# The first stage of a two-layer encoder step written as one list of steps over all engines

## The chip, the core and the metric

The kernel runs on one core of a Trainium2 chip. The core has engines that each take their own instructions in order: TensorE (PE in the profile; its weight loads are PEld), VectorE (DVE), ScalarE (ACT), GpSimd (POOL) and SyncE (SP). DMA transfers are issued by an engine and wait in that engine's queue (SPq, ACTq, POOLq). The metric is the device time of one execution in microseconds (us), the median over runs.

## The reference

One inference step of a two-layer encoder for 1024 prompt frames and 32 sample frames of width 1024, all in f32. Each layer makes modulation vectors from a condition, normalizes, mixes, and runs a feed-forward part:

```python
mod = jax.nn.silu(c) @ w_ada[i] + b_ada[i]              # 1024 -> 6 x 1024, for 2 conditions
sh1, sc1, gt1, sh2, sc2, gt2 = jnp.split(mod[:, None, :], N_MOD, axis=-1)
h = rmsnorm(x, g_norm[i, 0]) * (1 + sc1) + sh1
...
z = jax.nn.gelu(h @ w_in)                               # layer 0: spatial gating, 1024 -> 2 x 2048
u, v = jnp.split(z, 2, axis=-1)
v = rmsnorm(v, g_v)
...
x = x + gt1 * rmsnorm(mix, g_norm[i, 1])
h = rmsnorm(x, g_norm[i, 2]) * (1 + sc2) + sh2
f = jnp.square(jax.nn.relu(h @ ffn_w_up[i])) @ ffn_w_down[i]
x = x + gt2 * rmsnorm(f, g_norm[i, 3])
```

The stage that the change touches reads x, makes the first h of layer 0 out of it (with sh1 and sc1, the first 2048 of w_ada's 6144 columns), and begins the product of h with the v half of w_in.

## The kernel before

**Tiles.** The 1056 frames are nine blocks of 128 rows (the ninth has 32) in three tiles: blocks 0 to 2, 3 to 5, and 6 to 8. A tile lies transposed in `acc[t]`: model channels on the partitions, in eight groups of 128 (k = 0 to 7), frames along the row. Matmuls run on f32 values split in two: `wh` and `hh` are the rounded parts (type fp32r), `wl` and `hl` what is left. A product is three passes: hh by wh, hl by wh, hh by wl.

**The stream.** `stream` is the list of all loads from memory in the order in which they are issued, each 512 KB: blocks of x, pieces of w_ada and pieces of the weights. `issue()` (L395) sends them to SP's queue as long as slots are free, except that block 2 of x goes to ACT's queue; `stream_to(kind, key)` (L949) lets the kernel take up loads until the one named. The first 26 are three blocks of x, then four rounds q = 0 to 3 of four w_ada pieces (name `ada`) and one weight piece `("v", 0, q)`; x3 to x5 stand behind the weight piece of round 0.

**The first stage** stands in a part in which the program fixes the order itself (L991, `tc.manual_schedule()`). What it holds, for each engine:

- Small vectors (L180, `load_vectors`): g_norm, b_ada, pool_scale, g_v and the two conditions are loaded as rows through ACT's queue (tiles `row0` to `row2`) and turned on PE into columns (`csilT` for the conditions behind a Silu on ACT, `rowT` for the others).
- `x_squares` (L565): ACT squares a block and sums it, the sums go into `ssx`. `x_turn` (L580): PE transposes a block in two halves of four 128x128 transposes (`xT`), and VectorE or ACT (L588) copies each into `acc`.
- `do_ada_pe` (L477): PE multiplies a w_ada piece by the conditions (`ada0_0` to `ada0_7`; two pieces of four matmuls for each), VectorE turns the sums (`adas`), PE gathers them (`adat`, L459), and VectorE adds the bias (coefficients and shifts).
- `spread` (L715): from the sums of squares, VectorE makes the mean (`ms`), ACT takes a square root and VectorE a reciprocal (L722, L723), three VectorE steps refine it, ACT makes three diagonals (L730, `r_h`), and PE spreads them over the partitions (`pb`, L732).
- `apply`: for each k, VectorE multiplies `acc` by coefficient and factor (`mt`), ACT adds the shift and rounds (`hh`, L875), VectorE makes the rest (`hl`).
- `do_w`: ACT rounds a weight piece (`wh`, L422), VectorE subtracts (`wl`, L79).
- `early_mm(bs, q)` (L961, matmul at L973): the products of blocks bs by weight piece q into five PSUM tiles `pv0_0` to `pv0_4`, 120 matmuls in all.

The program writes these in whole pieces: all of tile 0's two k of a round, then `early_mm((0, 1, 2), q)`, then tile 1's two k, then `early_mm((3,), q)` and `early_mm((4,), q)`. Behind the last round, PE turns blocks 6 to 8, the third tile is normalized in the same way, and the stage of v follows: weight pieces `("v", 1, q)`, matmuls at L929 to L931, gelu (L941). `sgu_group` (L1142) belongs to the stage behind that: its small matrices `wt` and `bs` are loaded through SP's and ACT's queues as soon as a slot is free, the first two at the start of the program.

Of the kernel before, what the change touches and what calls it, by code (L numbers as in the profile page):

```python
# [34 lines left out]
def tile_stream_encoder_step(  # L35
# [154 lines left out]

    def turn_conditions():
        raw = vec_rows[2]
        nc.vector.memset(csil32, 0.0)
        act(out=raw[0:16, P : 2 * P], in_=raw[0:16, :P], func=AF.Silu)

        act(out=raw[0:16, 2 * P : 2 * P + 1], in_=epsT[0:16, :], func=AF.Sqrt)
        pt = ps_ms("csilT")
        nc.tensor.transpose(pt[:, 0:16], raw[0:16, P : 2 * P], ident[0:16, 0:16])
        nc.vector.tensor_copy(csil, pt[:, 0:16].rearrange("p (v k) -> p k v", v=NV))
        nc.vector.tensor_copy(csil32[:, :, 0:NV], csil)  # L200

    def turn_vectors():
        for raw, v in zip(vec_rows, vecs):
            n = v.shape[1]
            pt = ps_ms("rowT")
            nc.tensor.transpose(pt[:, :n], raw[:n, :P], ident[:n, :n])
            nc.vector.tensor_copy(v, pt[:, :n])
# [187 lines left out]
    def issue():  # L395
        while state["issued"] < len(stream):
# [22 lines left out]
    def do_w(key, r):  # L419
# [4 lines left out]
        if key == ("v", 0, 0):  # L424
            late_lo.append(lambda: tt(out=wl, in0=r, in1=wh.bitcast(F32), op=ALU.subtract))
        else:
            tt(out=wl, in0=r, in1=wh.bitcast(F32), op=ALU.subtract)


    late_lo = []  # L430
# [38 lines left out]

    pe_folds = []  # L470

    def do_ada_pe(l, sl, q, r):
        if q == 0:
            ada_acc[0] = ps_ms(f"ada{l}_{sl}")
        pa = ada_acc[0]
        for c in range(4):
            mm(  # L477
                pa[32 * c : 32 * c + 32, :256],
                csil32[:, 4 * q + c, :],
                r[:, c * 256 : (c + 1) * 256],  # L480
                start=q == 0,
                stop=q == 1,
                tile_position=(0, 32 * c),
                skip_group_check=True,
            )
        if q == 0:
            return
        s = t_m(f"adas{l}_{sl}")
        nc.vector.transpose(out=s[:, :256], in_=pa[:, :256])

        def fold():
            x = s[:, :256].rearrange("p (h a j) -> p a h j", h=2, a=4)
            pb = gather(f"adat{l}_{sl}", [x[:, a, :, 0:NV] for a in range(4)])
            ada_finish(
                l, sl // 4, 2 * (sl % 4), pb[:, : 2 * NV].rearrange("p (k v) -> p k v", v=NV)
            )

        pe_folds.append(fold)
# [73 lines left out]
    def x_turn(b, r):  # L572
# [3 lines left out]
        for half in range(2):  # L576
# [6 lines left out]
            dst = acc[t][:, half * 4 : half * 4 + 4, HALO + c0 : HALO + c0 + nr]  # L583
            src = pt[:, : 4 * nr].rearrange("p (a b) -> p a b", a=4)
            if half == 0 or t == 0:
                nc.vector.tensor_copy(dst, src)
            else:
                act(out=dst, in_=src, func=AF.Copy)  # L588
# [4 lines left out]
    def do_x(b, r):  # L593
        x_squares(b, r)
        if b < 3:
            x_turn(b, r)
        else:
            x_turns.append(lambda: x_turn(b, r))
# [10 lines left out]
    def stream_step():  # L609
# [10 lines left out]
        elif kind == "ada":  # L620
            if k < first_ada:
                do_ada_pe(*key, r)
            else:
                do_ada(*key, r, 256)
        else:
            do_x(key, r)
# [88 lines left out]
    def spread(t, ss, tag, out, dg):  # L715
# [6 lines left out]
        act(out=r0[:, :nb], in_=ms[:, :nb], func=AF.Sqrt)  # L722
        nc.vector.reciprocal(out=r0[:, :nb], in_=r0[:, :nb])  # L723
# [234 lines left out]
    early_ps = [(ps_dn if b < 3 else ps_up)(f"pv0_{b}") for b in range(5)]  # L958
    h0, h1, h2 = (first_norm(t) for t in range(NT))

    def early_mm(bs, q):  # L961

        wh, wl = witem[("v", 0, q)]
        for second in (False, True):
            for b in bs:
                t, c0 = b // 3, b % 3 * P
                tick(0.46 if second else 0.92)
                for k in range(2):
                    kb = 2 * q + k
                    a_h, a_l = hh[t][:, kb, c0 : c0 + P], hl[t][:, kb, c0 : c0 + P]  # L970
                    w = slice(k * 512, k * 512 + 512)
                    for a in (a_h,) if second else (a_h, a_l):
                        mm(  # L973
                            early_ps[b],
                            a,
                            (wl if second else wh)[:, w],
                            start=kb == 0 and a is a_h and not second,
# [696 lines left out]
```

## Time and profile before

| | |
|---|---|
| median of 3 runs | 2169.93 us (2169.7 to 2171.16) |
| the profiled execution: time | 2173.74 us |
| its span, from the first to the last instruction | 2171.7 us |
| TensorE clock granted, mean | 0.996 of full speed |
| busy over the span | PE 99%, PEld 96%, DVE 66%, ACT 45%, POOL 1% |
| bytes moved | 312.95 MB, mean 144 GB/s |

The page names groups of instructions by line, engine and operation, and by the tiles they write and read (`out<-in`); `x16` is a count. A view over stretches of time gives, for each engine, the busy time in the stretch with the number of instructions, and then the granted clock, the share of time in which the DMA engines were busy and their GB/s. The order of its engine columns is PE, PEld, DVE, ACT, POOL. A timeline gives for a window the start and the length of each group of instructions that stand together.

### The profile page before, as it was taken

To read this page: it belongs to the slowest core of one execution; us is meant where nothing else is said; L and a number is where in the kernel's file an instruction comes from. 1 tells how busy PE (TensorE), PEld (TensorE's weight loads), DVE (VectorE), ACT (ScalarE), POOL (GpSimd) and SP (SyncE) were. 2 spreads that over 40 slices of the span, in tenths; PEclk is the share of its full clock that TensorE was granted. 3 is DMA by queue.
4 is the path that set the end of the run, shared out by engine and by line. 5 is a ranking of instruction groups with operands and counts; after the bars stand their busy time and mean duration, and the time that the engine had idled before them with its cause. 6 is when DMAs were issued, how large, how long until landed. Compare 5 with 4: busy or idle time off the path is not lost.

```text
span 2171.7 us, 33210 instructions
## 1 busy us (share of the span) xinstructions
PE 2145.5 (99%) x13214; PEld 2078.1 (96%) x13214; DVE 1431.8 (66%) x2499; ACT 971.3 (45%) x1643; POOL 13.3 (1%) x30
## 2 busy tenths in 40 slices
PE   7999999999999999999999999999999999999998
PEld 5778899999999999999999999999999999999997
DVE  5688647566879548496747879869675554523377
ACT  4633422234447552323445566666555542313354
POOL 0000000000000000000000000000000000000001
PEclk9999999999999999999999999999999999999999
DMA  8386534343437454243645466565455552302255
GB/s 300 119 269 193 173 93 139 90 148 109 147 96 233 132 155 143 87 140 110 196 129 161 141 189 182 171 191 158 141 161 158 157 155 68 98 20 78 69 139 125
DMA packets 383262, 312.95 MB, mean 144 GB/s; under 512 B 39458, under 2 KB 346346, under 8 KB 383108
## 3 DMA queue, kind: packets, MB, share of 16 engines
q1 hardware_dynamic: 380452, 308.64, 46.8%
q8 instruction: 103, 1.69, 0.3%
q10 hardware_dynamic: 2144, 1.41, 0.2%
q0 software_dynamic: 512, 0.79, 0.1%
q14 instruction: 51, 0.42, 0.1%
HBM read 278.95 MB, written 31.84 MB: 143 GB/s over the span
## 4 chain that ended last, share of the span: by engine, by line
PE 93%; DVE 3%; DMA 2%; ACT 1%; issue 1%; ACTq 0%; DVEq 0%; SPq 0%
PE pg L902 11%; PE pg L903 11%; PE pg L904 11%; PE pf L902 11%; PE pf L904 11%; PE pf L903 11%; PE po L902 3%; PE po L903 3%; PE po L904 3%; PE pu L902 3%; PE pu L904 3%; PE pu L903 3%; PE pv L929 2%; PE pv L930 2%; PE pv L931 2%; PE pp L1532 1%
## 5 line engine op out<-in xcount | busy, mean ns | idle before, releaser
L902 PE MATMUL pg<-fh,wh_dn 128*128 128x384 f32 (+1 forms) x1536 | 495.8, 323 | 0.0
L902 PE MATMUL pf<-hh,wh_up 128*128 128x384 f32 (+1 forms) x1536 | 494.4, 322 | 0.0
L903 PE MATMUL pf<-hl,wh_up 128*128 128x384 f32 (+1 forms) x1536 | 493.1, 321 | 0.0
L904 PE MATMUL pf<-hh,wl_up 128*128 128x384 f32 (+1 forms) x1536 | 492.9, 321 | 0.2 <-DVE wl_up L79 0.2
L903 PE MATMUL pg<-fl,wh_dn 128*128 128x384 f32 (+1 forms) x1536 | 492.6, 321 | 0.4 <-DVE fl L79 0.4
L904 PE MATMUL pg<-fh,wl_dn 128*128 128x384 f32 (+1 forms) x1536 | 492.5, 321 | 0.0
L79 DVE TENSOR_TENSOR wl_up<-raw,wh_up 128x1024 fp32r<-128x1024 f32 x152 | 185.9, 1224 | 165.4 <-ACT wh_up L422 165.4
L902 PEld LDWEIGHTS pg<-fh,wh_dn 128*128 128x128 f32 x1536 | 288.3, 188 | 1.5 <-ACT fh L1121 0.6
L903 PEld LDWEIGHTS pg<-fl,wh_dn 128*128 128x128 f32 x1536 | 288.3, 188 | 1.5 <-DVE fl L79 0.7
L904 PEld LDWEIGHTS pf<-hh,wl_up 128*128 128x128 f32 x1536 | 288.6, 188 | 0.5 <-DVE wl_up L79 0.5
L903 PEld LDWEIGHTS pf<-hl,wh_up 128*128 128x128 f32 x1536 | 288.3, 188 | 0.4
L902 PEld LDWEIGHTS pf<-hh,wh_up 128*128 128x128 f32 x1536 | 288.2, 188 | 0.4
L904 PEld LDWEIGHTS pg<-fh,wl_dn 128*128 128x128 f32 x1536 | 288.3, 188 | 0.0
L422 ACT ACTIVATE wh_up<-raw 128x1024 fp32r<-128x1024 f32 x152 | 161.2, 1060 | 279.9 <-PE pf L903 213.6
L79 DVE TENSOR_TENSOR acc<-acc,pg 128x384 f32<-128x384 f32 (+1 forms) x336 | 174.2, 519 | 146.3 <-PE pg L904 145.7
L422 ACT ACTIVATE wh_dn<-raw 128x1024 fp32r<-128x1024 f32 x152 | 160.8, 1059 | 202.9 <-PE pg L903 170.6
L79 DVE TENSOR_TENSOR wl_dn<-raw,wh_dn 128x1024 fp32r<-128x1024 f32 x152 | 186.0, 1224 | 82.4 <-ACT wh_dn L422 82.2
L79 DVE SCALAR_TENSOR_TENSOR aa<-raw,csil,aa 128x512 f32<-128x512 f32 (+1 forms) x364 | 203.5, 623 | 8.0 <-DMA raw<-in_w_ada_dram 7.9
L1295 ACT ACTIVATE r<-pf 128x384 f32<-128x384 f32 (+1 forms) x192 | 86.6, 451 | 201.9 <-PE pf L904 199.2
L79 DVE TENSOR_TENSOR fl<-r,fh 128x384 fp32r<-128x384 f32 (+1 forms) x192 | 100.3, 523 | 85.4 <-ACT fh L1121 84.3
L902 PE MATMUL pu<-hh,wh_u 128*128 128x384 f32 (+1 forms) x384 | 125.8, 328 | 0.0
L902 PE MATMUL po<-ush,wh_o 128*128 128x384 f32 (+1 forms) x384 | 123.5, 322 | 0.0
(263 smaller groups left out, 2927.2 us busy)
## 6 DMA issues: line engine op xcount, KB each, us to landing
raw<-in_ffn_w_up_dram SPq DMA_DIRECT2D x152, 512.0 KB, 3.9
raw<-in_ffn_w_down_dram SPq DMA_DIRECT2D x152, 512.0 KB, 3.5
raw<-in_w_ada_dram SPq DMA_DIRECT2D x96, 512.0 KB, 4.3
raw<-in_sgu_w_in_dram SPq DMA_DIRECT2D x40, 512.0 KB, 4.4
xd<-acc SPq DMA_DIRECT2D x8, 1536.0 KB, 7.8
raw<-in_sgu_w_out_dram SPq DMA_DIRECT2D x24, 512.0 KB, 4.0
xo_r<-xd SPq DMA_DIRECT2D x32, 384.0 KB, 3.4
vd<-vt SPq DMA_DIRECT2D x32, 256.0 KB, 4.5
```

What stands on the lines that cost most here:

```text
L79: return op(out, *args, **kw)
L422: act(out=wh, in_=r, func=AF.Copy)
L902: mm(ps[:, :n], wh, rh, start=i == 0, stop=False)
L903: mm(ps[:, :n], wh, rl, start=False, stop=False)
L904: mm(ps[:, :n], wl, rh, start=False, stop=i == last)
L929: mm(ps[:m, :], a_h, wh[:, o : o + 512], start=k == 0, stop=False)
L930: mm(ps[:m, :], a_h, wl[:, o : o + 512], start=False, stop=False)
L931: mm(ps[:m, :], a_l, wh[:, o : o + 512], start=False, stop=k == KB - 1)
L1295: act(out=r[:, :n], in_=ps[:, :n], func=AF.Relu)
L1532: mm(ps[:, :n], wg[:, k, e * P : (e + 1) * P], A(t, 2 * g + k), start=k == 0, stop=k == 1)
```

## The change

The stage's pieces are broken into single steps, and the order of all of them is one list of words, `order`. Each word is a step with its numbers: `mt1_3` is mt of tile 1, k = 3; `hh` and `hl` likewise; `xT4_0` the first half of block 4's transposes and `xc4_0` its copy; `ada6_1` the second piece of ada 6; `g0_3`, `h0_3` and `l0_1` are the three passes hh by wh, hl by wh (for one k) and hh by wl (for two k) of block 0. A loop takes the words in order and calls the step's function, so that each engine's instructions stand in the order of the list. The list has 255 words (100 of them `g`, `h` and `l`) and ends with the squares of blocks 6 to 8; blocks 6 to 8 are turned behind it, as before.

Beside the order, these things change:

- `warm(12)` stands ahead of the list and four `warm` words in it (seven more matmuls): a 128x512 product of ones into a PSUM tile whose value nobody reads.
- x3 to x5 stand in the stream behind the weight piece of round 1 instead of round 0; block 2 of x goes to SP's queue like the others.
- g_norm, b_ada, pool_scale and g_v are loaded through GpSimd's queue; the conditions stay on ACT's.
- `spread` takes the inverse square root in one ACT instruction (Abs_reciprocal_sqrt), without VectorE's reciprocal. Two small ACT instructions ahead of their use take the functions' tables.
- The copies of the second halves of tile 1's and 2's blocks are on ACT, as before.
- `wt` and `bs` of `sgu_group` are issued only behind the load of `("v", 2, 3)`, and `bs` goes to SP's queue.

```diff
@@ load_vectors
-    def load_vectors(i, part):
+    def load_vectors(queue, i, part):
         at = sum(k for _, k in rows[i][: part.start])
         for ap, k in rows[i][part]:
-            nc.scalar.dma_start(vec_rows[i][at : at + k, :P], ap)
+            queue.dma_start(vec_rows[i][at : at + k, :P], ap)
...
@@ the stream
         add_w(*v_item(0, q))
-        if q == 0:
+        if q == 1:
             for b in range(3, 6):
                 add_x(b)
...
-                i = (nc.scalar if key == 2 else nc.sync).dma_start(
+                i = nc.sync.dma_start(
...
@@ spread
-        act(out=r0[:, :nb], in_=ms[:, :nb], func=AF.Sqrt)
-        nc.vector.reciprocal(out=r0[:, :nb], in_=r0[:, :nb])
+        act(out=r0[:, :nb], in_=ms[:, :nb], func=AF.Abs_reciprocal_sqrt)
...
@@ the first stage
-    def early_mm(bs, q):
...
+    def warm(n):
+        w = slot("pv0_2", lambda: ps_dn("pv0_2")) if "vec2" in held else slot("warm", lambda: ps_up("warm"))
+        for _ in range(n):
+            mm(w.rearrange("p (a b) -> p a b", a=4), onesr, fresh, start=True, stop=True)
...
+    def xT(b, half):
+        pt = slot(f"xT{b}_{half}", lambda: ps_ms(f"xT{b}_{half}"))
+        for i in range(4):
+            nc.tensor.transpose(
+                pt[:, i * P : (i + 1) * P], got("x", b)[:, half * 4 + i, :], ident
+            )
...
+    def high(b, k, part=None):
+        t, c0 = b // 3, b % 3 * P
+        tick(0.23)
+        w = witem[("v", 0, k // 2)][0][:, k % 2 * 512 : k % 2 * 512 + 512]
+        pv(b, (hl if part is None else part)[t][:, k, c0 : c0 + P], w)
+
+    def low(b, q):
+        t, c0 = b // 3, b % 3 * P
+        tick(0.46)
+        for k in range(2):
+            w = witem[("v", 0, q)][1][:, k * 512 : k * 512 + 512]
+            pv(b, hh[t][:, 2 * q + k, c0 : c0 + P], w)
...
+    order = """
+        silu xT0_0 xsq0 csilT xT0_1 xc0_0 csil xsq1 xT1_0 xc0_1 rowT0 xT1_1 vec0 xc1_0 xsq2 xT2_0
...
+        hh0_3 ms1 xc3_1 g2_3 hl0_3 g0_3 rs1 g1_3 xc4_1 xT5_0 nr1 ada6_0 xc5_0 dg1 ada6_1 ada2_0
...
     with tc.manual_schedule():
-        load_vectors(2, slice(0, 2))
+        load_vectors(nc.scalar, 2, slice(0, 2))
         issue()
-        load_vectors(2, slice(2, 4))
-        load_vectors(0, slice(0, 1))
-        load_vectors(1, slice(0, 1))
-        turn_conditions()
-        stream_to("x", 1)
-        turn_vectors()
...
+        load_vectors(nc.gpsimd, 0, slice(0, 1))
+        load_vectors(nc.gpsimd, 1, slice(0, 1))
+        load_vectors(nc.gpsimd, 2, slice(2, 4))
+        act(out=vec_rows[2][64:80, P : P + 1], in_=epsT[64:80, :], func=AF.Silu)
+        nc.vector.memset(csil32, 0.0)
+        warm(12)
+        for step in order.split():
+            name = step if step in steps else step.rstrip("0123456789_")
+            steps[name](*(int(i) for i in step[len(name) :].split("_") if i))
+        for b in (6, 7, 8):
+            x_turns.append(lambda b=b: x_turn(b, got("x", b)))
...
@@ sgu_group
-        nc.sync.dma_start(wt, sgu_w_s[0, g])
         bb = sgu.tile([P, P], F32, tag="bs", bufs=2, name=f"bs{g}")
-        nc.scalar.dma_start(bb, sgu_b_s[0, g].partition_broadcast(P))
+        with tc.issue_after(loads[("v", 2, 3)]):
+            nc.sync.dma_start(wt, sgu_w_s[0, g])
+            nc.sync.dma_start(bb, sgu_b_s[0, g].partition_broadcast(P))
```

**Where instructions now stand.** In the rows below, names are the program's with a buffer number at the end, `out<-in`, and x4 means four in a row. The first place is PE's start of the program. Before:

```order
L198 MATMUL csilT_187<-ident_80,row2_114 128x16
L580 MATMUL xT0_0_192<-ident_80,x_rows0_121 128x128 x4
L580 MATMUL xT0_1_198<-ident_80,x_rows0_121 128x128 x4
L580 MATMUL xT1_0_205<-ident_80,x_rows0_121 128x128 x4
L580 MATMUL xT1_1_211<-ident_80,x_rows0_121 128x128 x4
L206 MATMUL rowT_217<-ident_80,row0_112 128x64
L206 MATMUL rowT_220<-ident_80,row1_113 128x96
L206 MATMUL rowT_223<-ident_80,row2_114 128x40
```

And after:

```order
L928 MATMUL warm_181<-ones_85 128x512 x12
L961 MATMUL xT0_0_195<-ident_80,x_rows0_121 128x128 x4
L934 MATMUL csilT_201<-ident_80,row2_114 128x16
L961 MATMUL xT0_1_203<-ident_80,x_rows0_121 128x128 x4
L961 MATMUL xT1_0_212<-ident_80,x_rows0_121 128x128 x4
L946 MATMUL rowT0_218<-ident_80,row0_112 128x64
L961 MATMUL xT1_1_220<-ident_80,x_rows0_121 128x128 x4
L961 MATMUL xT2_0_228<-ident_80,x_rows0_121 128x128 x4
L946 MATMUL rowT1_233<-ident_80,row1_113 128x96
```

Twelve products of ones now stand first, the conditions' transpose stands behind the first half of block 0, and g_norm (`row0`) ahead of the second half of block 1.

The second place is POOL's start of the program, where the identity matrix is made. Before:

```order
masks.py:197 MEMSET ident_80 128x128
masks.py:199 ISA
masks.py:199 AFFINE_SELECT ident_80<-ident_80 128x128
L1172 MEMSET vl0_2_2652 128x256
L1172 MEMSET vl1_2_2899 128x256
```

And after:

```order
masks.py:197 MEMSET ident_80 128x128
L183 DMA row0_112<-in_g_norm_dram 64x128
masks.py:199 ISA
masks.py:199 AFFINE_SELECT ident_80<-ident_80 128x128
L183 DMA row1_113<-in_b_ada_dram 96x128
L183 DMA row2_114<-in_pool_scale_dram 8x128
L183 DMA row2_114<-in_sgu_g_v_dram 16x128
```

The load of g_norm now stands between the two halves of the identity, and the three others behind it.

The third place is SP's order of loads, from its start. Before (`x_rows1` are blocks 3 to 5):

```order
L410 DMA x_rows0_121<-in_x_prompt_dram 128x1024 x2
L414 DMA raw3_139<-in_w_ada_dram 128x4x256
L414 DMA raw4_141<-in_w_ada_dram 128x4x256
L414 DMA raw5_143<-in_w_ada_dram 128x4x256
L414 DMA raw6_145<-in_w_ada_dram 128x4x256
L414 DMA raw7_147<-in_sgu_w_in_dram 128x2x512
L410 DMA x_rows1_122<-in_x_prompt_dram 128x1024 x3
L414 DMA raw11_152<-in_w_ada_dram 128x4x256
```

And after, from the first weight piece on (what stands ahead of it is as before, with block 2 of x among the first):

```order
L396 DMA raw7_142<-in_sgu_w_in_dram 128x2x512
L396 DMA raw8_144<-in_w_ada_dram 128x4x256
L396 DMA raw9_146<-in_w_ada_dram 128x4x256
L396 DMA raw10_148<-in_w_ada_dram 128x4x256
L396 DMA raw11_150<-in_w_ada_dram 128x4x256
L396 DMA raw12_152<-in_sgu_w_in_dram 128x2x512
L392 DMA x_rows1_122<-in_x_prompt_dram 128x1024 x3
L396 DMA raw16_157<-in_w_ada_dram 128x4x256
```

The four w_ada pieces of round 1 and its weight piece now stand ahead of x3 to x5.

The fourth place is ACT around the second tile's squares. Before:

```order
L875 ACTIVATE hh0_0_0_300<-mt0_0_0_302,shift_119 128x384
L875 ACTIVATE hh0_0_0_300<-mt0_1_0_304,shift_119 128x384
L565 ACTIVATE xsq_124,ssx_117<-x_rows1_122 128x8x128 x3
L722 ACTIVATE r0_h0_1_334<-ms_h0_1_333 128x3
L588 ACTIVATE acc1_73<-xT3_1_348 128x4x128
```

And after:

```order
L1075 ACTIVATE wh_v_0_1_374<-raw12_152 128x1024
L1051 ACTIVATE hh0_0_0_313<-mt0_2_366,shift_119 128x384
L511 ACTIVATE xsq_124,ssx_117<-x_rows1_122 128x8x128 x3
L1051 ACTIVATE hh0_0_0_313<-mt0_3_377,shift_119 128x384
L538 ACTIVATE acc1_73<-xT3_1_399 128x4x128
L1007 ACTIVATE r0_h0_1_432<-ms_h0_1_426 128x3
```

The second weight piece and hh of k = 2 now stand ahead of the squares of x3 to x5, and hh of k = 3 right behind them.

More of the change, by code (lines that the diff above doesn't have):

```diff
@@ new lines, in adas, with adat, cf @@
+    def adas(sl):
+        s = slot(f"adas{sl}", lambda: t_x(f"adas0_{sl}", [P, 256]))
+        nc.vector.transpose(out=s, in_=held[f"ada{sl}"][:, :256])
+    def adat(sl):
+        x = held[f"adas{sl}"].rearrange("p (h a j) -> p a h j", h=2, a=4)
+        held[f"adat{sl}"] = gather(f"adat0_{sl}", [x[:, a, :, 0:NV] for a in range(4)])
+    def cf(sl):
+        ada_finish(
+            0,
+            sl // 4,
+            2 * (sl % 4),
+            held[f"adat{sl}"][:, : 2 * NV].rearrange("p (k v) -> p k v", v=NV),
+        )
@@ new lines, in dg, with pb @@
+    def dg(t):
+        cp = slot(f"dg{t}", lambda: t_c(f"r_h0_{t}"))
+        for b in range(3):
+            act(
+                out=cp[:, b * P : (b + 1) * P],
+                in_=ident,
+                func=AF.Copy,
+                scale=held[f"nr{t}"][:, b : b + 1],
+            )
+    def pb(t):
+        p = slot(f"pb{t}", lambda: ps_ms(f"pb_h0_{t}"))
+        for b in range(3):
+            c = slice(b * P, (b + 1) * P)
+            mm(p[:, c], ones, held[f"dg{t}"][:, c], start=True, stop=True)
@@ new lines, in low @@
+    def low(b, q):
[4 more added lines that the diff above has]
+            pv(b, hh[t][:, 2 * q + k, c0 : c0 + P], w)
+    steps = {
+        "silu": silu,
+        "csilT": csilT,
+        "csil": csil_copy,
+        "rowT": rowT,
+        "vec": vec,
+        "xsq": xsq,
+        "xT": xT,
+        "xc": xc,
+        "ada": ada,
+        "adas": adas,
+        "adat": adat,
+        "cf": cf,
+        "ms": ms,
+        "tab": tab,
+        "rs": rs,
+        "nr": nr,
+        "dg": dg,
+        "pb": pb,
+        "r": spread_copy,
+        "mt": mt,
+        "hh": hi,
+        "hl": lo,
+        "wh": whi,
+        "wl": wlo,
+        "g": lambda b, k: high(b, k, hh),
+        "h": high,
+        "l": low,
+        "warm": warm,
+    }
```

260 lines of the change are left out of this document (147 added, 113 removed).

## The prediction

> **What bounds the kernel.** I read the busy shares, then the same by stage, then who waits for whom on PE.
>
> ```profile
> PE 2145.5 (99%) x13214; PEld 2078.1 (96%) x13214; DVE 1431.8 (66%) x2499; ACT 971.3 (45%) x1643; POOL 13.3 (1%) x30
> ```
> ```profile
> 0.00:30.00 30.00, 20.42 (x116) 14.95 (x116) 14.03 (x59) 15.03 (x29) 0.69 (x6) 0.89 0.94 333
> 30.00:70.00 40.00, 37.48 (x276) 26.57 (x276) 24.31 (x49) 16.28 (x29) 0.00 (x0) 0.96 0.50 171
> 70.00:90.00 20.00, 18.31 (x87) 14.41 (x85) 10.16 (x23) 16.30 (x34) 0.00 (x0) 1.00 0.50 158
> 90.00:200.00 110.00, 110.00 (x495) 87.20 (x494) 93.65 (x228) 42.38 (x90) 0.00 (x0) 1.00 0.69 220
> ```
> ```profile
> PE csilT L198 <- ACT row L194: 6.6, 1, 6.6
> PE pv L973 <- ACT hh L875: 1.9, 1, 1.9
> PE adat L459 <- DVE adas L489: 1.7, 1, 1.7
> PE pv L930 <- DVE wl_v L79: 1.6, 1, 1.6
> PE psp L1213 <- DMA vl<-vd: 0.7, 1, 0.7
> ```
>
> In the stretch table the first figure after the length is PE's busy time; the last three are granted clock, DMA share and GB/s. PE is the bound: from 90 us it is busy 110.00 of 110.00, and its longest wait behind the first stage is 0.7 us. So whatever time the first stage ends earlier should reach the end of the kernel whole, and I look only at when PE leaves that stage. Before 70 us PE is idle 9.6 + 2.5 us.
>
> A part of its busy time there is slow work too:
>
> ```profile
> 6.79 3.68 PE L580 MATMUL xT<-ident,x_rows 128*128 128x128 f32 x16
> 13.40 3.45 PE L477 MATMUL ada<-raw,csil 128*32 128x256 f32 x32
> 27.08 2.04 PE L580 MATMUL xT<-ident,x_rows 128*128 128x128 f32 x16
> 45.53 1.93 PE L477 MATMUL ada<-raw,csil 128*32 128x256 f32 x32
> ```
> ```profile
> 10.00:12.00 2.00, 1.86 (x9) 1.09 (x8) 1.52 (x5) 1.34 (x4) 0.00 (x0) 1.00 0.42 106
> 12.00:14.00 2.00, 2.00 (x15) 1.44 (x17) 1.18 (x2) 0.00 (x0) 0.00 (x0) 1.00 0.89 305
> 22.00:24.00 2.00, 2.00 (x6) 1.53 (x5) 0.21 (x2) 1.73 (x5) 0.00 (x0) 0.50 1.10 389
> 26.00:28.00 2.00, 2.00 (x14) 1.68 (x14) 0.28 (x1) 0.00 (x0) 0.00 (x0) 0.97 1.08 389
> 36.00:38.00 2.00, 1.96 (x13) 1.59 (x14) 1.72 (x4) 0.00 (x0) 0.00 (x0) 0.59 1.09 385
> ```
>
> The same 16 transposes take 3.68 and 2.04 us, the same 32 ada matmuls 3.45 and 1.93: a factor of 1.8. The clock column prints 0.50 at 22 us and 0.59 at 36 us; at 7 and 13 us it prints 1.00, but the durations say half speed there too. Loads run at 385 to 389 GB/s once going, with a hole at 10 to 14 us.
>
> **The end of the stage before.**
>
> ```profile
> 64.11 1.52 PE L973 MATMUL pv<-wl_v,hh 128*128 128x512 f32 x6
> 68.20 2.04 PE L580 MATMUL xT<-ident,x_rows 128*128 128x128 f32 x16
> ```
>
> Transposing blocks 6 to 8, the first work behind the 120 early pv matmuls, starts at 68.2 us. I need the same instant for the list. A pv matmul costs (1.52 - 0.39)/5 = 0.228 us in a stream (0.39 is the length of a single record, five spacings are left).
>
> **Loads, which gate the list's first half.** The 512 KB transfers queue behind each other on SP, so position in the queue gives the landing.
>
> ```profile
> 19.60 1.97 SPq L414 DMA_DIRECT2D raw<-in_sgu_w_in_dram  x1
> ```
> ```profile
> raw<-in_sgu_w_in_dram SPq DMA_DIRECT2D x1, 512.0 KB, 9.4
> ```
> ```profile
> SPq L414 <- DMA row<-in_c_sample_dram: 2.7, 1, 2.7
> SPq L414 <- DMA x_rows<-in_x_prompt_dram: 2.0, 1, 2.0
> ```
>
> Before, the 16th is the weight piece v(0,1): 19.6 + 9.4 = 29.0 us. In the list the 16th is x5, the last block of the second tile. The hole at 10 to 14 us, against 390 GB/s, is 2 x (390 - 106) + 2 x (390 - 305) = 738 KB, 1.9 us; it stands behind SP's waits for slots that ACT's small loads held. With those on GpSimd's queue and the two bs loads (128 KB, 0.3 us) gone, x5 should land at 29.0 - 1.9 - 0.3 = 26.8 us. Bounds: 29.0 (the hole stays), 25.7 (the start quickens by another 1.1).
>
> **From x5 to the end of the list.** On ACT, hh0_3 stands behind xsq5; on PE, g2_3, g0_3, g1_3 stand ahead of xT5_0.
>
> ```profile
> 55.37 0.18 ACT L565 ACTIVATION_READ_ACCUMULATOR xsq<-x_rows 128x1 f32 x1
> 60.10 1.15 ACT L875 ACTIVATE hh<-mt,shift 128x384 fp32r<-128x384 f32 x2 [4.55 <-DVE mt L79]
> 54.42 1.04 ACT L565 ACTIVATE xsq<-x_rows 128x1024 f32<-128x1024 f32 x1
> 47.28 0.22 PE L459 MATMUL adat<-adas,squares 128*32 128x4 f32 x8
> 76.60 0.94 PE L732 MATMUL pb_h<-r_h,ones 128*128 128x128 f32 x6
> ```
>
> That is 1.04 + 0.18 + 1.15/2 + 3 x 0.228 = 2.5 us: PE reaches xT5_0 at 29.3. Is PE itself there by then? Ahead of xT5_0 the list has 27 pv (6.2 us), 40 transposes at 2.04/16 (5.1), eight ada steps of 1.93/4 (3.9), four adat (0.9), pb (0.9), four small transposes (0.8 at 0.2) and seven warm matmuls (1.6): 19.4 us. The opening burst of 12 warm matmuls at the cold spacing, 0.228 x 1.8 = 0.41, ends near 1.5 + 4.9, say 6.5 us. So PE would be there at 25.9 and has 3.4 us to spare: the loads decide, and the warm matmuls in the gaps cost nothing under that cover.
>
> From xT5_0 on PE has 93 pv (21.2), eight ada steps (3.9), eight transposes (1.0), four adat (0.9) and pb (0.9): 27.9 us, with weights and vectors landing ahead of it. How tightly does PE run such mixed rows? One round before:
>
> ```profile
> 45.60 1.85 PE ada L477 x30
> 55.64 1.85 PE ada L477 x30
> ```
>
> 10.04 us a round; its 30 pv, four ada steps and two adat sum to 6.8 + 1.9 + 0.4 = 9.1, so 9% is lost, a good part at one hand-over from hh to hl. The list spreads such hand-overs; I take 6% (1.6 us), with 0 to 9% as ends. VectorE could be the later one:
>
> ```profile
> 59.46 1.14 DVE L79 SCALAR_TENSOR_TENSOR mt<-acc,coef,r_h 128x384 f32<-128x384 f32 x2
> 58.22 1.23 DVE L79 TENSOR_TENSOR wl_v<-raw,wh_v 128x1024 fp32r<-128x1024 f32 x1
> ```
>
> From mt1_0, some 33 us, it has 24 products mt and hl at 1.14/2 (13.7), two wl (2.5) and small work of about 3: 19 us. So wl3 is ready near 52, ahead of the five last pairs that need it.
>
> Stage end: 29.3 + 27.9 + 1.6 = 58.8 us against 68.2: 9.4 us earlier.
>
> **The rest, part by part.**
>
> ```profile
> 71.33 0.18 DVE L723 RECIPROCAL r_h<-r_h 128x3 f32<-128x3 f32 x1 [0.32 <-ACT r_h L722]
> 73.06 1.28 ACT L941 ACT_TABLE_LOAD   x1
> 86.67 0.50 PE L930 MATMUL pv<-wl_v,hh 128*128 128x512 f32 x1 [1.59 <-DVE wl_v L79]
> ```
>
> The reciprocal of the third tile goes: 0.2 us of the chain by way of the table load to the weights that PE waits 1.59 us for. That wait moves with the stage end, since its loads start off weights split behind it; I count 0.2 and keep up to 1.6 for the low end. The table loads are the same number (the early ones stand under the wait for x), so 0. The ten later bs loads on SP are ten more issues in a queue whose PE consumers wait nowhere in that stage: 0. Behind the stage PE, DVE and ACT run the same instructions, so no giving back is costed.
>
> Sum: -9.4 - 0.2 = -9.6 us. The profiled execution's span is 2171.7 and its time 2173.74; the runs' median, 2169.93, lies 3.8 below that. I subtract from the median: 2160.3, rounded to 2160.5.
>
> **Rivals.** First, the burst does not hold the clock. PE ran without a break from 6.6 us and was still slow at 13.4; it was fast at 27 us, after six microseconds of unbroken pv. So 12 warm matmuls may not be enough, or the transposes behind them let it fall back. Each cold microsecond of work loses 1 - 1/1.8 = 0.44: cold until 16 us, PE comes to xT5_0 at 25.9 + 4.2 = 30.1 (+0.8); cold until 26.4, at 25.9 + 8.8 = 34.7 (+5.4). That is 2161.3 to 2165.9, middle 2163.5. Against it: the transposes at 27.08 stayed fast.
>
> [...]
>
> Second, the hole in the loads stays or another opens: x5 at 29.0, +2.2, 2162.7.
>
> Third, on the other side: the vectors come late by GpSimd's queue. PE takes its rows in order, and rowT0 (g_norm) stands ahead of half the first tile's transposes, due near 8 us.
>
> ```profile
> out_dram<-turned POOLq DMA_DIRECT2D x16, 48.0 KB, 3.0
> row<-in_b_ada_dram ACTq DMA_DIRECT2D x1, 48.0 KB, 4.2
> bs<-in_sgu_b_s_dram ACTq DMA_DIRECT2D x1, 64.0 KB, 8.6
> ```
>
> Issued at 1 to 3 us, they land at 4 to 7 by the first two rows and at 10 to 12 by the third, which PE's 3.4 us still cover. Past 11.5 us each microsecond costs one: no gain from 21 us, and at 26 us the kernel takes 2175. GpSimd also writes one load between the two halves of the identity, with some four microseconds of cover.
>
> Fourth, the gain is given back at 90 to 130 us, where VectorE is close to full: 2168 to 2171. Its work and PE's shift together, so I doubt it.
>
> **Chances.** Forecast 0.46 (own range 2158 to 2162.5), cold clock 0.23, late loads 0.12, given back 0.09, vectors late 0.10. Low end: x5 at 25.7 (-1.1), no loss on PE (-1.6) and half of the 1.6 us wait: 2157. High end: cold to 26.4 with 9% lost is 2166.7, and the case that is given back begins at 2168, which I take. No change is within 0.2% (4.3 us, about what a measurement of this kernel can tell): 2165.6 to 2174.3. Faster: 0.46 + 0.12 + most of the cold case + the vectors late by a little = 0.78; same (given back, the rest of the cold case) 0.15; slower 0.07.
>
> **What would show it.** Right: transposes of blocks 0 to 2 at 0.13 us each, loads without a hole before 40 us, PE without waits over half a microsecond from 30 us, blocks 6 to 8 transposed at 58 to 60 us, and from there to the end the same span as before, 2103. Wrong: PE waiting on rowT0, clock 0.5 behind 10 us, or PE waiting for hl or hh behind 35 us, which would say that VectorE or ACT and not PE is the list's bound.

## The result and the profile after

The changed kernel takes 2161.95 us (median of 6 runs, 2161.22 to 2162.67) against 2170.94 for the kernel before (6 runs). The ratio is 0.9959, 95% interval 0.9946 to 0.9971: 9.0 us or 0.41% faster. A repeat on another occasion gave 0.9955 (0.9943 to 0.9968). The profiled execution took 2161.22 us with a span of 2159.4.

In the same four stretches as before (PE's busy time first, the granted clock, DMA share and GB/s last):

```profile
0.00:30.00 30.00, 28.02 (x200) 18.00 (x204) 17.82 (x68) 17.38 (x33) 2.87 (x10) 1.00 1.00 361
30.00:70.00 40.00, 39.91 (x265) 30.08 (x258) 22.66 (x46) 23.31 (x44) 0.00 (x0) 1.00 0.46 156
70.00:90.00 20.00, 18.74 (x83) 15.20 (x82) 15.71 (x45) 13.25 (x33) 0.00 (x0) 1.00 0.72 223
90.00:200.00 110.00, 110.00 (x495) 87.23 (x494) 95.76 (x223) 40.30 (x80) 0.00 (x0) 1.00 0.73 229
```

PE is busy 28.02 of the first 30 us (20.42 before), the clock column prints 1.00 throughout (the opening burst still runs slow, 5.49 us for its twelve products), and the loads no longer pause: the stretches 10 to 12 and 12 to 14 us, which moved 106 and 305 GB/s before, now read

```profile
10.00:12.00 2.00, 2.00 (x21) 1.05 (x23) 2.00 (x7) 0.21 (x2) 0.00 (x0) 1.00 1.09 387
12.00:14.00 2.00, 2.00 (x28) 1.03 (x28) 1.06 (x7) 0.99 (x3) 0.00 (x0) 1.00 1.06 396
```

PE's longest waits of the whole kernel, and the stations of the first stage on PE's timeline (start, length, and in brackets the idle time ahead):

```profile
PE warm L928 <- DVE ones L129: 1.4, 1, 1.4
PE pv L875 <- DVE wl_v L79: 1.3, 1, 1.3
PE pv L1089 <- ACT hh L1051: 0.6, 1, 0.6
```
```profile
1.36 5.49 PE L928 MATMUL warm<-ones 128*128 128x512 f32 x12 [1.36 <-DVE ones L129]
6.65 0.86 PE L961 MATMUL xT<-ident,x_rows 128*128 128x128 f32 x4
...
28.45 0.97 PE L1089 MATMUL pv<-wh_v,hh 128*128 128x512 f32 x3 [0.58 <-ACT hh L1051]
29.25 0.60 PE L961 MATMUL xT<-ident,x_rows 128*128 128x128 f32 x4
...
58.01 2.04 PE L526 MATMUL xT<-ident,x_rows 128*128 128x128 f32 x16
```

Between the first product at 1.36 us and the end of the stage, PE waits once, 0.58 us, for hh0_3. Block 5 is transposed at 29.25 us (31.00 before) and the stage ends, in the sense of the prediction, at 58.01 us (68.20 before): 10.2 us earlier. Further on the two traces are 10.7 us apart at the first product of u, 11.0 at the first of the feed-forward part, 11.7 at its last, and 12.3 at the end of the span. So in this pair of profiles nothing is given back. The medians are 9.0 us apart; the profile of before came from an execution 2.8 us above its median.

### The profile page after: what moved, and what is told of

It reads as the page before. It is cut to its first block, busy times and chain, and to the rows that moved or that the text cites. A ratio compares the mean times of both kernels' runs of the same rounds, so it can differ in the third digit from the quotient of the medians.

```text
span 2159.4 us, 33252 instructions
## 1 busy us (share of the span) xinstructions
PE 2145.1 (99%) x13233; PEld 2076.5 (96%) x13233; DVE 1429.8 (66%) x2496; ACT 971.0 (45%) x1644; POOL 15.3 (1%) x34
## 4 chain that ended last, share of the span: by engine, by line
PE 96%; DVE 2%; DMA 1%; ACT 1%; issue 0%; DVEq 0%; SPq 0%
PE pg L847 11%; PE pf L847 11%; PE pf L849 11%; PE pf L848 11%; PE pg L848 11%; PE pg L849 11%; PE po L847 3%; PE po L848 3%; PE po L849 3%; PE pu L847 3%; PE pu L849 3%; PE pu L848 3%; PE pv L874 2%; PE pv L875 2%; PE pv L876 2%; PE psp L1353 1%
```

## The experiments

The stage end is read from each profile; it comes out alike in repeats (58.01 and 57.88 us for the changed kernel). The time is less sharp: between the stage end and the last feed-forward product these profiles spread over 2089.1 to 2093.1 us, with the same instructions.

| kernel | stage end, us | time, us | ratio to before (95%) |
|---|---|---|---|
| before | 68.20 | 2169.93 to 2172.70 (medians on each occasion) | 1 |
| changed | 58.01 | 2161.95 | 0.9959 (0.9946 to 0.9971) |
| changed, repeat | 57.88 | 2162.70 | 0.9955 (0.9943 to 0.9968) |
| no products of ones | 57.35 | 2161.60 | 0.9955 (0.9942 to 0.9968) |
| vectors on ACT's queue | 59.01 | 2164.60 | 0.9967 (0.9955 to 0.9979) |
| old load plan | 61.90 | 2166.20 | 0.9972 (0.9962 to 0.9982) |
| x3 to x5 early | 64.41 | 2168.57 | 0.9984 (0.9976 to 0.9993) |
| old order behind x5 | 62.68 | 2168.11 | 0.9981 (0.9971 to 0.9990) |
| pairs of w_ada, no ones | 58.46 | 2163.83 | 0.9958 (0.9945 to 0.9970) |
| the same, hh0_3 earlier | 58.36 | 2163.92 | 0.9960 (0.9946 to 0.9974) |
| before + burst | 68.73 | 2171.83 | 1.0000 (0.9992 to 1.0009) |
| before + load plan | 65.38 | 2171.06 | 0.9995 (0.9985 to 1.0004) |
| before + ones in all gaps | 65.24 | 2171.98 | 0.9998 (0.9989 to 1.0007) |
| before + both | 65.04 | 2171.77 | 0.9999 (0.9989 to 1.0008) |

### Without the products of ones

```diff
-        warm(12)
         for step in order.split():
...
-        ... ada4_0 ms0 xc2_0 rowT2 xc2_1 rs0 warm1 ada4_1 nr0 adas4 dg0 vec2 warm2 ada0_0 ...
+        ... ada4_0 ms0 xc2_0 rowT2 xc2_1 rs0 ada4_1 nr0 adas4 dg0 vec2 ada0_0 ...
```

> The changed kernel without any of its 19 products of ones (the 12 ahead of the list and the seven in it). The clock theory: without them PE starts cold, as in the kernel before, where the transposes took 0.23 us each until 10 us and ada matmuls 0.108 us until 17 us; cold until 16 us costs about 4 us of PE time and cold until 26 us about 8.8 us, of which PE's wait of 0.58 us at 28 us, the 1.7 us that the burst itself takes beyond the landing of block 0 (its products end at 6.65 us, the squares of block 0 start at 5.00 us) and the 1.7 us of the seven others are given back: the stage ends at 58 to 63 us instead of 58.0 and the kernel is 0 to 5 us slower, likeliest 1 to 3. The rival, that the loads alone decide the first half and the clock is hidden: 58.0 us within 0.3 and the same time.

Measured: 57.35 us, half a microsecond earlier than with them, and the same time. That is nearer to the rival, but not for its reason. PE's start without the burst:

```profile
4.56 1.08 PE L961 MATMUL xT<-ident,x_rows 128*128 128x128 f32 x4 [4.56 <-DMA x_rows<-in_x_prompt_dram]
5.58 0.28 PE L934 MATMUL csilT<-ident,row 16*128 16x16 f32 x1
5.79 1.97 PE L961 MATMUL xT<-ident,x_rows 128*128 128x128 f32 x8
...
7.99 1.75 PE L961 MATMUL xT<-ident,x_rows 128*128 128x128 f32 x8
...
9.65 0.60 PE L961 MATMUL xT<-ident,x_rows 128*128 128x128 f32 x4
```

The first eight of a row take 1.97 us, the last four 0.60: the clock is full from about 9.4 us, after less than five microseconds of transposes alone. With the burst it is full at about 7.2. The two kernels without ones further down agree: their last four transposes take 0.60 us (from 10.43 us) and 0.73 (from 9.96). The burst buys two microseconds of clock and ends 2.1 us after block 0 could have been started (6.65 against 4.56). The other seven products are no gain either: this kernel's gaps in PE's row, up to 0.8 us, do not lower the clock.

The extra half microsecond comes by ACT. Its rows around the squares of blocks 3 to 5, changed kernel first, then without the ones (`wh_v`: second weight piece, `hh`: hh0_2, `xsq`: block 5's square, `hh`: hh0_3):

```profile
21.96 1.06 ACT L1075 ACTIVATE wh_v<-raw 128x1024 fp32r<-128x1024 f32 x1 [4.45 <-DMA x_rows<-in_x_prompt_dram]
23.87 0.62 ACT L1051 ACTIVATE hh<-mt,shift 128x384 fp32r<-128x384 f32 x1 [0.85 <-DVE shift L79]
...
26.74 1.06 ACT L511 ACTIVATE xsq<-x_rows 128x1024 f32<-128x1024 f32 x1
...
27.80 0.60 ACT L1051 ACTIVATE hh<-mt,shift 128x384 fp32r<-128x384 f32 x1
```
```profile
22.13 1.06 ACT L1075 ACTIVATE wh_v<-raw 128x1024 fp32r<-128x1024 f32 x1 [5.83 <-DMA x_rows<-in_x_prompt_dram]
23.10 0.60 ACT L1051 ACTIVATE hh<-mt,shift 128x384 fp32r<-128x384 f32 x1
...
25.96 1.06 ACT L511 ACTIVATE xsq<-x_rows 128x1024 f32<-128x1024 f32 x1
...
27.02 0.60 ACT L1051 ACTIVATE hh<-mt,shift 128x384 fp32r<-128x384 f32 x1
```

In the changed kernel hh0_2 waits 0.85 us for a shift that hangs on PE's ada 5; without the ones PE is there earlier and the wait is gone. The three squares follow each other without a pause, so block 5 had landed by 25.96 us, and in the changed kernel ACT came to it 0.8 us late. Without the ones ACT's row is unbroken from the second weight piece at 22.13 us to hh0_3, so PE waits for that row there and not for block 5.

### The load plan, in two steps

The vectors alone:

```diff
-        load_vectors(nc.gpsimd, 0, slice(0, 1))
-        load_vectors(nc.gpsimd, 1, slice(0, 1))
-        load_vectors(nc.gpsimd, 2, slice(2, 4))
+        load_vectors(nc.scalar, 0, slice(0, 1))
+        load_vectors(nc.scalar, 1, slice(0, 1))
+        load_vectors(nc.scalar, 2, slice(2, 4))
```

> The changed kernel with g_norm, b_ada, pool_scale and g_v back on ACT's queue. The theory of the load hole: SP's loads wait again for slots behind ACT's small loads, 1 to 2 us of the transfers are lost at 10 to 14 us, x5 is squared at 28 to 28.5 us instead of 26.7, and the stage ends 1 to 2 us later (59 to 60 us). The rival, that the hole came from the two bs loads or from block 2 on ACT's queue and not from the vectors: 58.0 us within 0.3.

Measured: 59.01 us, 1.0 later, at the near end of what was expected. The waits of SP's queue name the cause (two of their rows):

```profile
SPq L396 <- DMA row<-in_g_norm_dram: 1.4, 1, 1.4
SPq L396 <- DMA row<-in_b_ada_dram: 1.0, 1, 1.0
```

SP's big loads stand behind vectors that are on ACT's queue; in the changed kernel no such line is there. The whole old plan but for the place of x3 to x5:

```diff
-                i = nc.sync.dma_start(
+                i = (nc.scalar if key == 2 else nc.sync).dma_start(
...
-        with tc.issue_after(loads[("v", 2, 3)]):
-            nc.sync.dma_start(wt, sgu_w_s[0, g])
-            nc.sync.dma_start(bb, sgu_b_s[0, g].partition_broadcast(P))
+        nc.sync.dma_start(wt, sgu_w_s[0, g])
+        nc.scalar.dma_start(bb, sgu_b_s[0, g].partition_broadcast(P))
```

> The changed kernel with the old load plan but for the place of x3 to x5: vectors on ACT's queue, block 2 of x on ACT's, the small matrices of the later stage loaded as soon as a slot is free. The vectors alone, on ACT's queue, moved the stage end from 58.0 to 59.0. If the sum of the prediction (a hole of 1.9 us and 0.3 us for two bs loads) holds: 60.0 to 60.5 us and 2 to 2.5 us more time than the changed kernel. If the small loads only use the queue's spare time: 59.0 as with the vectors alone.

Measured: 61.90 us, 3.9 later, more than either case. In its stretches the hole is back, and the clock falls in it; the row in the second fence is PE's wait:

```profile
10.00:14.00 4.00, 2.35 (x20) 0.80 (x16) 2.29 (x8) 2.87 (x8) 0.00 (x0) 1.00 0.89 251
14.00:18.00 4.00, 2.33 (x22) 1.95 (x22) 0.33 (x2) 0.00 (x0) 0.00 (x0) 0.66 1.05 378
```
```profile
15.66 1.08 PE L972 MATMUL ada<-raw,csil 128*32 128x256 f32 x8 [3.31 <-DMA raw<-in_w_ada_dram]
```

Against 392 GB/s in the changed kernel, 251 over 4 us is 1.4 us of transfers. PE rests 3.31 us for a w_ada piece and starts it 2.5 us later than in the changed kernel (15.66 us against 13.13). Then the eight matmuls of that piece take 1.08 us instead of 0.64, and at the first pv PE is 3.9 us late (21.13 us against 17.24), as it is at the end of the stage: the hole costs its length and a stretch at half clock behind it. How the 2.9 us beyond the vectors' 1.0 divide between block 2 of x on ACT's queue and the small matrices was not tried.

### x3 to x5 early

```diff
-        if q == 1:
+        if q == 0:
             for b in range(3, 6):
                 add_x(b)
```

> The changed kernel with x3 to x5 behind the first weight piece of the stream, as before; the list is unchanged. If the list's order needs the w_ada pieces of round 1 first, PE waits about 4 us (three transfers of 1.35 us) for the first of them at 16.7 us and for the second weight piece at 25 us; with 0.58 us of cover and x5 no longer late, the stage ends 2 to 4 us later (60 to 62 us). The rival, that the place of x is worth nothing because the loads in all decide: 58.0 us within 0.5.

Measured: 64.41 us, 6.4 later, beyond the 2 to 4 that were expected. The first wait came as foreseen and the second, for the weight piece, did not come; what was not foreseen is what the first one starts:

```profile
20.34 1.08 PE L972 MATMUL ada<-raw,csil 128*32 128x256 f32 x8 [4.11 <-DMA raw<-in_w_ada_dram]
21.35 2.07 PE L1089 MATMUL pv<-wh_v,hh 128*128 128x512 f32 x4
```
```profile
20.00:22.00 2.00, 1.66 (x10) 0.79 (x11) 0.00 (x0) 0.00 (x0) 0.00 (x0) 0.50 1.09 386
22.00:24.00 2.00, 2.00 (x12) 0.80 (x10) 0.00 (x0) 0.00 (x0) 0.00 (x0) 0.50 1.07 398
24.00:26.00 2.00, 2.00 (x12) 0.89 (x11) 0.45 (x1) 0.47 (x1) 0.00 (x0) 0.50 1.08 386
```

After 4.11 us of rest PE works at half clock until past 26 us: it is 3.7 us late where the rest ends (20.34 us against 16.67 in the changed kernel) and 6.4 us late at block 5 (35.66 against 29.25). So the list and the place of x3 to x5 belong together: with this list the old place costs most of the gain. What the place is worth by itself, with an order made for it, was not tried.

### Parts of the change in the kernel before

Three kernels put the burst, the load plan, and products of ones in all of PE's gaps into the old order.

```diff
+        fresh = onesr.unsqueeze(1).broadcast_to([P, 4, P])
+        pw = early_ps[4].rearrange("p (a b) -> p a b", a=4)
+        for _ in range(12):
+            mm(pw, onesr, fresh, start=True, stop=True)
```

> The kernel before with only the burst of 12 products of ones ahead of its first stage. If the cold clock was what held the stage back: transposes and ada matmuls of the first 17 us at full speed, the stage ends 3 to 4 us earlier (64 to 65 us instead of 68.2). If waits between engines and for loads stood behind the cold work: under 1 us earlier, PE is idle instead, and the clock falls back to half in the gaps.

Measured: 68.73 us and ratio 1.0000. The burst alone does nothing. PE is through with its cold work earlier (the first sixteen transposes take 2.10 us instead of 3.68), waits 3.74 us for the next w_ada piece, and is cold again for what follows. Three stretches of this kernel, and the same of the kernel with ones in all gaps:

```profile
14.00:18.00 4.00, 1.18 (x16) 0.50 (x20) 0.00 (x0) 0.57 (x2) 0.00 (x0) 0.87 1.04 393
18.00:22.00 4.00, 2.40 (x30) 1.84 (x22) 1.97 (x6) 1.79 (x3) 0.00 (x0) 0.50 1.05 398
22.00:26.00 4.00, 3.79 (x8) 2.77 (x9) 2.28 (x3) 3.94 (x8) 0.00 (x0) 0.50 1.04 358
```
```profile
14.00:18.00 4.00, 4.00 (x38) 2.44 (x37) 0.24 (x1) 0.58 (x2) 0.00 (x0) 1.00 1.05 417
18.00:22.00 4.00, 3.81 (x25) 2.47 (x24) 3.12 (x9) 3.37 (x6) 0.00 (x0) 1.00 1.05 384
22.00:26.00 4.00, 4.00 (x23) 3.35 (x22) 1.75 (x7) 2.63 (x7) 0.00 (x0) 1.00 1.08 391
```

```diff
@@ before + load plan
-        load_vectors(2, slice(2, 4))
-        load_vectors(0, slice(0, 1))
-        load_vectors(1, slice(0, 1))
+        load_vectors(nc.gpsimd, 0, slice(0, 1))
+        load_vectors(nc.gpsimd, 1, slice(0, 1))
+        load_vectors(nc.gpsimd, 2, slice(2, 4))
...
+        with tc.issue_after(loads[("v", 2, 3)]):
@@ before + ones in all gaps
+        fill(12)
         turn_conditions()
...
+            fill(14)
+            stream_to("ada", (0, q, 0))
+            fill(2)
```

> The kernel before with only the changed load plan: g_norm, b_ada, pool_scale and g_v through GpSimd's queue, block 2 of x through SP's, the small matrices of the later stage behind the load of v(2,3); x3 to x5 and the order of the work as before. If the hole in the loads at 10 to 14 us is worth its 1.9 us and the two bs loads 0.3 us to the stage: stage end at 66.0 instead of 68.2 us, 1.5 to 2.5 us less time. The rival, that in the old order PE, VectorE and ACT wait for each other and not for loads from 20 us on: under 0.7 us.

> The kernel before with 44 products of ones: the burst of 12, then 14, 2, 7, 3 and 6 in the gaps in which PE waited (for the third w_ada piece, for hh, for the diagonals, for the turned sums of ada 5), so that PE never rests. The order theory: the clock stays granted from 7 us on, and with the burst alone the kernel ended its stage at 68.7 because the clock fell to half for 10 us from 17 to 27; at full speed those twelve pv matmuls and what stands ahead of them take some 3 us less, so stage end 65 to 66.5 us; what is left to the 58.0 of the list is order. The rival, that the whole difference between the two kernels is the clock: stage end near 60 us. The other, that waits behind the cold work stay anyway: 68 us.

> Both of the two edits above: the old order with the new load plan and PE kept busy by products of ones in its gaps. If the parts add: 63 to 64.5 us for the stage end, and 5 to 6.5 us between that and the list's 58.0 are the order of the steps. If loads and clock together were the whole gain: 58 to 60 us.

Measured: 65.38, 65.24 and, for both, 65.04 us. Each ends its stage about 3 us earlier than the profile of before, and the second edit adds almost nothing to the first. In the kernel with the load plan alone, the rows show another clock and no shorter wait for a load:

```profile
11.64 1.09 PE L580 MATMUL xT<-ident,x_rows 128*128 128x128 f32 x8
12.66 1.93 PE L477 MATMUL ada<-raw,csil 128*32 128x256 f32 x32
```

In the profile of before, the same eight transposes read

```profile
11.50 1.97 PE L580 MATMUL xT<-ident,x_rows 128*128 128x128 f32 x8
```

and the same 32 matmuls take 3.45 us; the profile names no wait of PE for a load in the stage. The kernel with the load plan is 1.5 us ahead at the first `adat` (15.16 us against 16.66), 1.6 at block 5 (29.41 against 31.00), and 2.8 at the end of the stage, since the half clock at 36 to 40 us does not come. So its 2.8 us come with the clock of that execution; that the new loads brought that clock is not shown.

In the kernel with both edits the ones hold up PE, because their number fits the gaps of the old loads:

```profile
12.23 3.47 PE L990 MATMUL pv<-ones 128*128 128x512 f32 x14
18.44 0.49 ACT L893 ACTIVATE r_h<-pb_h 128x384 f32<-128x384 f32 x1 [4.06 <-PE pb_h L732]
```

With the load plan alone, PE works on the w_ada pieces at that time, ACT waits 0.58 us for `pb_h` instead of 4.06, and its first hh starts at 17.72 us instead of 19.78. So 65.04 us is no floor of the old order: I estimate from these 2.1 us that it could reach some 63 us with full clock, new loads and no ones in the way, which was not tried. Of the 7.0 us between 65.04 and the list, about 5 are left to the order, with the place of x3 to x5 that belongs to it. From block 5 to the end of the stage all three kernels take 36.0 us, at a clock of 1.00 and without a wait of PE for a load. The rival that all of it is the clock, or loads and clock together, does not fit that, and the next kernel tests it with the loads and the clock of the list.

In time these three show less than their 3 us: 0.2 to 1.1 us, with intervals that reach 2.4 us for the latter two and 3.3 for the first. Part of the reason is on record. Of the 30 executions of the kernel before that were timed beside them, 14 had a mean granted clock of 0.998 and a median of 2171.0 us, and 16 had a lower clock and a median of 2173.0 us. The profile of before has 0.996, and the kernel with ones in all gaps has 0.998 in all ten executions, with a median of 2172.0 us. So the half clock that costs the stage of before some of its 68.20 us is not in every execution; at which time the stage ends in the others, no profile here shows. PE's longest wait behind the stage is 1.3 to 1.4 us in these three, and 1.6 in the kernel before.

### The old order behind x5

```diff
-        hh0_3 ms1 xc3_1 g2_3 hl0_3 g0_3 rs1 g1_3 xc4_1 xT5_0 nr1 ada6_0 xc5_0 dg1 ada6_1 ada2_0
-        adas6 pb1 xT5_1 r1 ada2_1 xc5_1 mt1_0 l1_1 wh2 adas2 h2_3 h1_3 mt1_1 l2_1 hh1_0 ada7_0 ...
+        hh0_3 ms1 xc3_1 g2_3 hl0_3 g0_3 rs1 g1_3 xc4_1 xT5_0 nr1 xc5_0 dg1 pb1 xT5_1 r1 xc5_1
+        h0_3 h1_3 h2_3 l0_1 l1_1 l2_1 mt1_0 hh1_0 hl1_0 mt1_1 hh1_1 hl1_1 g3_0 h3_0 g3_1 h3_1 ...
```

> The changed kernel with its list up to the first transposes of block 5 (word xT5_0) and behind that the same steps in the old order: all passes of tile 0, then both k of tile 1, then blocks 3 and 4, with four w_ada pieces in a row in each round. PE has the same 27.9 us of work behind xT5_0; the list runs it in 28.8. With loads and clock made equal the old order ran its 31.1 us in 36.0 from that point, 4.9 us lost. If that loss is the order behind x5, the stage ends at 61 to 63 us. The rival, that what counts is how much is done ahead of x5 and VectorE and ACT can follow any order then: 58 to 59 us.

Measured: 62.68 us, within the expected 61 to 63, and the rival's 58 to 59 is out. From xT5_0 (28.88 us) PE needs 33.8 us for the 27.9 us of work that the list runs in 28.8, at a clock of 1.00 throughout. (The 31.1 us and 4.9 us lost in the expectation are 31.4 and 4.6 when counted again.) Its waits in the stage, in that kernel:

```profile
PE pv L1089 <- ACT hh L1051: 2.6, 4, 0.7
...
PE pv L1089 <- DVE hl L79: 0.6, 4, 0.2
```

The first row holds the 0.58 us for hh0_3 ahead of xT5_0, which the list has too. Behind xT5_0, PE stands three times for 0.7 us until ACT has made the hh of the second k of a pair, and four times for 0.2 us until VectorE has made an hl. These waits and one of 0.2 us for the diagonals are 2.9 us; the remaining 3.0 of the 5.9 us lost are short pauses, none of them named.

### Two attempts at more

```diff
-        ... xT5_0 nr1 ada6_0 xc5_0 dg1 ada6_1 ada2_0 adas6 pb1 xT5_1 r1 ada2_1 ... ada7_0 ... ada7_1 ...
+        ... xT5_0 nr1 ada6_0 xc5_0 dg1 ada6_1 ada2_0 ada2_1 adas6 pb1 xT5_1 r1 ... ada7_0 ada7_1 ...
@@ in the second kernel also
-        ... xsq5 h2_2 h1_2 h0_2 hh0_3 ms1 ...
+        ... hh0_3 xsq5 h2_2 h1_2 h0_2 ms1 ...
```

> The changed kernel without its 19 products of ones and with the w_ada pieces of a pair next to each other (ada2_1 behind ada2_0, ada7_0 ahead of ada7_1, ada3_0 ahead of ada3_1). A piece alone between pv matmuls takes about 0.3 us more than one in a row (0.57 us to the next instruction instead of 0.48, and 0.66 instead of 0.46 for the pair of pv behind it). Against 57.35 us without the products of ones: 0.5 to 0.8 us earlier, 56.6 to 56.9, if these hand-overs are PE's own price; 57.3 if PE only waits elsewhere then.

> The same with hh0_3 on ACT ahead of the square of block 5 instead of behind it. PE's wait of 0.6 to 0.7 us for hh0_3 goes; the chain from block 5's square to the first product of tile 1 comes 0.6 us later, which has about 0.6 us of room. Stage end 0 to 0.7 us earlier than with the pairs alone; 0.6 us later at most if that chain has no room. In the time of the whole kernel neither this nor the pairs is likely to be told from no change.

The repeat of the changed kernel, which ran beside them, had this expectation:

> The changed kernel itself once more, as the measure for the others on this chip: stage end 58.0 us within 0.7 (loads land a little earlier or later), time 0.35 to 0.5% under the kernel before.

Measured: 57.88 us for the repeat, 58.46 for the pairs and 58.36 with hh0_3 ahead of block 5's square as well. Both are later than the 57.35 without ones, by 1.1 and 1.0 us; the first lies outside both cases of its expectation. In time neither can be told from the changed kernel. The hand-overs between kinds that I wanted to save are small against what moving ada2_1 forward costs: its piece has not landed, and the diagonals of tile 1, which stand behind it on PE, come late. PE in the kernel with pairs:

```profile
31.23 0.64 PE L972 MATMUL ada<-raw,csil 128*32 128x256 f32 x8 [0.55 <-DMA raw<-in_w_ada_dram]
31.79 0.94 PE L1031 MATMUL pb_h<-r_h,ones 128*128 128x128 f32 x6
...
35.30 0.73 PE L1089 MATMUL pv<-wh_v,hh 128*128 128x512 f32 x2 [0.56 <-DVE mt L79]
```

With hh0_3 earlier, PE reaches xT5_0 at 27.49 instead of 28.64 us, and all of it is taken back at the same loads. Nothing here beats the changed kernel beyond its uncertainty; leaving the ones out is simpler and not slower.

## Why the prediction was right, and where its steps were off

**The end of the stage.** 58.8 us was forecast and 58.0 measured, 9.4 us earlier and 10.2; the kernel is 9.0 us faster by the medians where 9.6 was forecast from 2169.93. It rests on PE's being the bound behind the stage, and that holds: no wait there is longer than the 1.3 us for `wl_v`, which was 1.6 before (the prediction's "0.7 us" for the longest wait behind the stage leaves that row out), and the nine runs of the list order themselves in time as in stage end, but for neighbours within 0.2 us of stage end. The 68.2 us of before come from one execution at a granted clock of 0.996, and the sum took the difference off a median whose executions often had a higher one. How much of 9.4 and 10.2 us is that clock in a median execution was not measured, so that 9.0 came so near 9.6 may be partly luck.

**PE at xT5_0.** 29.3 us forecast, 29.25 measured, but two steps behind that number were off. PE was not there at 25.9 with 3.4 us to spare; it had 0.58. The row of PE is full from 6.65 to 27.9 us with what I had priced at 19.4 us by rates within long streams: among short groups a w_ada piece takes 0.57 to the next instruction instead of 0.48, and a pair of pv behind it 0.57 to 0.66 instead of 0.46. And it was not the landing of x5 that came last. It had landed by 26.0 us or sooner, 0.8 before my 26.8, and ACT's row was late by as much through the wait for the shift. The two errors cancelled, so the agreement of 29.25 with 29.3 is luck. The sentence that the ones in the gaps cost nothing under the cover fails by half a microsecond for the same reason.

**From there to the end.** 27.9 us of work was right, and the loss, taken as 1.6 us out of 0 to 2.5, was 0.9. VectorE's last wl is ready at 50.4 us, forecast near 52.

**Where the 10.2 us come from**, which the prediction did not split. Block 5 is reached 1.75 us earlier. By then the list has done nine pv, four w_ada pieces and two adat more and one pb less: 2.05 + 1.93 + 0.44 - 0.94 = 3.5 us. Behind it the old order lost 5.8 us (37.2 us for 102 pv, twelve pieces, six adat and eight transposes, 23.3 + 5.8 + 1.3 + 1.0 = 31.4) and the list 0.9: 4.9 us. With the clock at 1.00 the old order still lost 36.0 - 31.4 = 4.6. About 2.8 of the 10.2 us hang on the clock of the profiled execution of before: by so much the kernel with the old order and the new load plan is ahead of it, with the same work on PE.

**The loads.** The hole went as forecast, for the reason named (SP's waits for small loads on ACT's queue). Its price, 2.2 us, was too small by 1.7: PE's rest of 3.31 us was followed by a stretch at half clock, 1.4 of the 3.9 us, for which the sum has no term.

**The rivals.** The burst held the clock (the two rows of eight transposes behind it took 1.35 and 1.09 us, such a row in the kernel before 1.97), so the cold-clock case did not come, but neither of its sides was right: without the burst the list is not slower. The list leaves no rest of more than 0.8 us, and at none of them did the clock fall; where a load made it rest for 3.31 or 4.11 us, it did. The transposes did not let the clock fall back, and in the kernel without the burst it came to full speed with nothing but transposes ahead: 0.25 us for each of the first four and 0.14 for the last ones. The vectors on GpSimd's queue were in time, as the first rows gave it (3.0 and 4.2 us) and not the third: from issue to landing they took

```profile
row<-in_b_ada_dram POOLq DMA_DIRECT2D x1, 48.0 KB, 5.4
row<-in_g_norm_dram POOLq DMA_DIRECT2D x1, 32.0 KB, 4.7
```

and no transpose of them waited.

**Behind the stage.** The 0.2 us for the reciprocal were not tried by themselves. 2103 us was forecast from there to the end, "the same span as before". The profile gives 2101.4, the repeat 2103.1, before 2103.5. Given back at 90 to 130 us was nothing: PE is busy 110.00 of 110.00 from 90 to 200 us in both.

## What to carry to other kernels

Where an engine is full behind a stage, a stage is worth what it frees at its end, and that can be read from one instruction's start in the profile, far more sharply than from the time. Read it from more than one execution where the clock can differ between them: the kernel before and its copy with the new load plan got two different clocks for the same work on PE (0.996 and 0.997 in the mean; the same eight transposes took 1.97 and 1.09 us). Write a start-up stage as one list over all engines with the matrix engine's row full of small independent steps: with whole blocks of one operand it stood at hand-overs, 0.7 us for hh alone, at a clock of 1.00 and without a wait for a load. Keep small loads off a queue that the big ones wait on (the vectors on ACT's queue cost 1.0 us of the stage), and do not add matmuls to warm the clock before it is shown that the real work does not do it (the stage ended at 57.35 us without them, at 58.01 with them).

## What was not expected of the hardware

The clock of PE fell after a rest of 3.3 to 4.1 us and stayed at half for 3.4, 6.8 or 10.2 us (changed kernel with the old load plan, with x3 to x5 early, before with the burst), by the clock column once, twice and three times 3.4 us. In the kernel before, it fell in a rest of 1.85 us (ended at 19.77 us) and stayed at half for 6.8 us from 19.3 us, and again for 3.4 us from 36.4 us. The half clock at 36 us follows rests of 1.0, 0.3 and 1.7 us between 29 and 36 us. But the same three rests stand in the old order with the new load plan (the last ends at 34.45 us) and with the burst (37.80 us), and there the clock stayed at 1.00.

The start differs in the same way. The kernel before began with transposes at 6.6 us and was cold until 15.9 us. With the new load plan it has the same row on PE and began at 6.8 us; its first sixteen transposes take 3.68 us in both, but the next eight take 1.09 us instead of 1.97. So pauses in PE's row cannot be all that decides; what else does, is not shown here.
